# Opening of a fused pooling trunk: stores queued later, loads in another order, the second half's tiles one by one, small root steps on GpSimd

## The chip, the cores and the metric

The kernel runs on one core of a Trainium2 chip. TensorE (PE) multiplies, with its weight loads on a queue of their own (PEld); VectorE (DVE) and ScalarE (ACT) work on tiles in SBUF and PSUM; GpSimd (POOL) issues some DMAs and can do small arithmetic; SyncE (SP) issues the other DMAs. Each engine takes its own instructions in order, and waits are by semaphore. The metric is the device time of one execution in microseconds; lower is better. Three runs of the kernel before gave 965.98, 966.9 and 967.35 us, a median of 966.9.

## The reference

With DEPTH = 1 only the pooling mixer runs. Its input x is (1, 4096, 1024) in float32.

```
normed = x * rsqrt(mean(x*x, axis=-1) + 1e-6) * norm_w
u, gate = split(normed @ in_w, 2)                      # in_w 1024 x 2048
pooled  = trailing means of u, windows 2/4/8/16 for its four channel groups, minus u
mixed   = per group: pooled @ group_w + group_b        # four maps of 256 x 256
y       = mixed * scale * silu(gate)
h       = x + y @ out_w                                # out_w 1024 x 1024
out     = h * rsqrt(mean(h*h, axis=-1) + 1e-6) * final_norm_w
```

## The kernel before

**Weights.** The group map is linear and commutes with pooling, so the kernel folds it into the first matrix: `fold` (L329) multiplies the u columns of in_w by the group maps, 8 matmul chunks of 16 matmul records each, and writes the result out of PSUM scaled by norm_w (L346). Four chunks (group pair 0) stay in SBUF as `v0` and `v1`; the four chunks of group pair 1 go to DRAM (`wvd`, L955) and are read again much later.

**Products.** Each big product is one level of a seven-product scheme (P1 to P7): the 1024-wide contraction and the tokens are cut in halves, and combinations of the halves are multiplied. A block is 1024 tokens, in two halves of 512. `xs[b]` holds four pairs of input tiles: "11" and "12" are the first half (two contraction halves), "21" and "22" the second, each of two tiles of 128 x 1024. Float32 accuracy comes from two float32r parts: `split` (L153) writes the high part by ACT and the low part by DVE, and `mm3` (L509) makes three matmuls of each pair of parts. There are 48 matmuls in a product of the stages "a" and "b". The list of steps is a P1 P2 P6 P7 P5 P4 P3 for four blocks, then "b" likewise for the other half of the columns, then "o" with out_w.

**The opening** (L897 to L1023) is written out by hand and then ordered by a scheduler, so the lists of instructions on each engine are fixed in the built program. It holds 14 warming matmuls (L900), the 8 chunks of `fold`, P1 and P2 of block 0 on the raw input, and the row statistics of block 0. The statistics go as follows: x is read a second time by rows (`load_row` L354, four tiles for each half); ACT squares and sums them (`square_row` L361, L365); `stats` (L370) makes the mean square; `rsqrt` (L187) makes its inverse root, by an ACT square root, a DVE reciprocal and one Newton step of four small DVE instructions; `spread_rs` (L383) splits the result in two parts `hl`, multiplies an identity by them on DVE (L389) and lets PE spread them over all partitions by two matmuls with ones into bank 7 (L396); ACT copies that into `rstd` (L401). The scratch tile of L389 is w[P7][0], the place of one of P7's weights. The first half's spread stands inside P1 and the second half's inside P2 in PE's list. P1's and P2's results are multiplied by rstd when they leave PSUM (L623); P6 is the first product that needs normalized input, of both halves: `normalize_raw` (L497) for "11" and "12", L984 for "21" and "22", then `form_in` (L460) takes differences, `split_step` splits them, and P6 can run. Tiles of the first block that are needed again are saved to DRAM by POOL's queue (L429 and L501, eight stores, beside four of `wvd`).

**Buffers.** `st` and `vt` are rings of 128 x 1024 tiles. `early` and `early5` are views of the places of weights that come later (P4 and P3, and P5). SP's DMAs use eight semaphores in turn, so that a DMA waits at least for the one eight places ahead of it.

Lines that the change and the prediction touch: `rsqrt` L187, `fold` L329, `spread_rs` L383, `split_halves` L423, `normalize_raw` L497, `mm3` L509, `product_in` L518, the opening L917 to L989, and the first turn of the main loop, L1074.

Of the kernel before, what the change touches and what calls it, by code (L numbers as in the profile page):

```python
# [10 lines left out]
F32 = mybir.dt.float32  # L11
# [49 lines left out]
def kernel(  # L61
# [125 lines left out]
    def rsqrt(dst, tmp, ms):  # L187

        nc.scalar.activation(tmp, ms, AF.Sqrt)
        nc.vector.reciprocal(out=dst, in_=tmp)  # L190
# [137 lines left out]

    def fold(q, k, g, r, ps2, o, on_vector=False):  # L329

        for kk in range(2):
            for j in range(2):
                for t in range(2):
                    nc.tensor.matmul(  # L334
                        ps2[kk][:, j * 256 : (j + 1) * 256],
                        r[:, kk, 2 * j + t, :],
                        g[:, 2 * j + t, :],
                        start=(t == 0),
                        stop=(t == 1),
                    )  # L340
            if on_vector:
                last = nc.vector.tensor_scalar(
                    out=o[:, kk], in0=ps2[kk], scalar1=norm_c[k + kk], scalar2=None, op0=ALU.mult
                )
            else:
                last = nc.scalar.activation(o[:, kk], ps2[kk], AF.Copy, scale=norm_c[k + kk])  # L346
        give(r)
        return last

# [30 lines left out]
    def store_rs(b, half, rs):  # L380
        nc.sync.dma_start(out=rd[b][half][0].rearrange("(p j) -> p j", j=4), in_=rs)

    def spread_rs(half, rs):  # L383

        hl = small.tile([P, 2, 4], F32R, tag="hl", name=f"hl{half}")
        split(hl, rs)
        r = w[P7][0]
        for s in range(2):
            nc.vector.tensor_tensor(  # L389
                out=r[:, s, 0].rearrange("p (a j) -> p a j", j=4),  # L390
                in0=ident.rearrange("p a b -> p (a b)")[:, 0:P].unsqueeze(2).to_broadcast([P, P, 4]),
                in1=hl[:, s].bitcast(F32).unsqueeze(1).to_broadcast([P, P, 4]),
                op=ALU.mult,
            )
        for s in range(2):
            nc.tensor.matmul(  # L396
                banks[7], ones, r[:, s, 0], start=s == 0, stop=s == 1, skip_group_check=True
            )
        if half == 0:
            rstd[0] = take()  # L400
        copy(rstd[0][:, half], banks[7])  # L401
# [16 lines left out]
    def next_op(pattern, **sizes):  # L418
        t = ops[turn[0] % 4]
        turn[0] += 1  # L420
        return t.rearrange(pattern, **sizes)

    def split_halves(us, saved=None, by_pool=False):  # L423
        ts = []
        for h, u in enumerate(us):
            t = next_op("p (s a b) -> p s a b", s=2, a=2)
            split(t, u)
            if saved is not None:
                (nc.gpsimd if by_pool else nc.scalar).dma_start(out=saved[h], in_=u)  # L429
            ts.append(t)  # L430
        return ts
# [28 lines left out]
    def form_in(q, b, i):  # L460
# [6 lines left out]
        elif i == P6:  # L467
            s["2"] = [take(pool=early if q == 0 and b == 0 else None) for _ in range(2)]
            for h in range(2):
# [15 lines left out]
    def split_in(q, b, i):  # L485
# [9 lines left out]
        return t  # L495

    def normalize_raw(i):  # L497
# [9 lines left out]


    def mm3(ps, lt, r, start, stop):  # L509

        for n, (a, b) in enumerate(((lt[0], r[0]), (lt[0], r[1]), (lt[1], r[0]))):
            nc.tensor.matmul(  # L512
                ps, a, b, start=start and n == 0, stop=stop and n == 2, skip_group_check=True
            )

    bank_of = {P1: "x", P2: "x", P6: "y", P5: "y", P3: "y", P7: "v", P4: "v"}

    def product_in(i, t, sets, by_bank, between=None):  # L518
        ps = sets[bank_of[i]]
# [3 lines left out]
        for n, (h, ct) in enumerate(halves):  # L523
            if between and n in between:
                between[n]()
            c = slice(ct * P, (ct + 1) * P)
            for kk in range(2):
                mm3(
                    ps[ct],
                    (w[i][h][:, 0, kk, c], w[i][h][:, 1, kk, c]),  # L530
                    (t[h][:, 0, kk], t[h][:, 1, kk]),
                    i in (P1, P7) and h == 0 and kk == 0,
                    h == 1 and kk == 1,
                )

# [331 lines left out]

    def run(n, between=None):
        kind, b, i = steps[n]
# [4 lines left out]
        else:  # L874
            product_in(i, split_up.pop(n), sets, i == P1, between)
            evict_in(b, 0 if kind == "a" else 1, i, sets)
# [40 lines left out]
    for n, (h, k) in enumerate(chunks):  # L917
        if k < 4:
            o = v0[h] = take(pool=early)
        else:  # L920
            o = v1[h] = take()
        fold(0, k, gw[0], ru[0, k], banks[2 * (n % 2) : 2 * (n % 2) + 2], o)
        ru[1, k] = load_wut(1, k)
        if n == 0:
            load(0)
            g0.append(load_rows(in_w, 2, D))
            split_scaled(w[P1][0], g0[0], pair(norm_c, 0, 0))
        elif n == 1:
            split_step(0)
        elif n == 2:  # L930
            split_scaled(w[P1][1], g0[1], pair(norm_c, 1, 0))
# [20 lines left out]
    for n, (h, k) in enumerate(chunks):  # L952
        o = take(pool=early if n < 2 else early5)
        fold(1, k, gw[1], ru[1, k], banks[2 * (n % 2) : 2 * (n % 2) + 2], o)
        nc.gpsimd.dma_start(out=wvd[k // 2], in_=o)  # L955
        give(o)
        if n < 2:
            second_side(n)
            for j in range(2 * n, 2 * n + 2):
                square_row(0, 0, j)  # L960
            if n == 1:
                with tc.high_priority():
                    rs[0] = stats(0, 0)
        else:
            for j in range(2 * n - 4, 2 * n - 2):
                square_row(0, 1, j)
    give(gw[1])
    load(2)
    with tc.high_priority():
# [17 lines left out]
    run(1)  # L987
    normalize_raw(P2)
# [62 lines left out]
    for n in range(2, len(steps)):  # L1051
# [101 lines left out]
```

## Time and profile before

| what | value |
|---|---|
| median of three runs | 966.9 us |
| the profiled execution, its own time | 964.39 us |
| its span (first to last instruction) | 962.6 us |
| PE busy in the span | 949.7 us (99%), 4190 matmul records |
| DVE busy | 748.4 us (78%) |
| ACT busy | 453.0 us (47%) |
| POOL busy | 6.7 us, 16 instructions |
| granted TensorE clock, mean | 0.997 |
| one 128x512 matmul, L512, mean record | 389 ns |
| share of the busy 16 DMA engines, 10 to 60 us | 1.01 to 1.03 in each 10 us |
| the same, 70 to 80 us | 0.10 |

PE's records overlap, so the mean record is longer than the distance from one matmul to the next. PE is busy 844.55 of the 850 us from 110 to 960 us; most of what it stands idle lies in the first 62 us and after the last matmul. The trace shows 1.5 us of idle PE before its first matmul, and then waits of 1.2 us and 2.1 us in the opening. In the span's first 60 us the DMA engines have no pause, and from 40 to 80 us DVE has none either (9.92 of 10, then 10.00 of each 10 us).

### The profile page before, as it was taken

The page shows a single profiled execution, that of the slowest core. Times are in us where ns is not written, and L with a number is a line of the kernel's source. Part 1 is how long each engine was busy: PE and PEld are TensorE (multiplying, and loading weights), DVE is VectorE, ACT ScalarE, POOL GpSimd, SP SyncE. Part 2 cuts the span into 40 slices and gives each one's busy share as a digit, 9 for nine tenths or more (in the row PEclk, how much of TensorE's full clock was granted, in tenths as well). Part 3 has the DMA queues.
Part 4 walks back from the last instruction along what each step waited for, and adds up shares of the span by engine and source line. Part 5 has one row for each costly group of instructions (what it writes and reads, how often), then busy time and mean ns, then how long its engine had stood idle before and what let it go on. Part 6 is the DMA issues. An engine that isn't in the chain of part 4 may idle for free.

```text
span 962.6 us, 11058 instructions
## 1 busy us (share of the span) xinstructions
PE 949.7 (99%) x4190; PEld 785.5 (82%) x4190; DVE 748.4 (78%) x919; ACT 453.0 (47%) x677; POOL 6.7 (1%) x16
## 2 busy tenths in 40 slices
PE   9999999999999999999999999999999999999996
PEld 8778888888888888888888888888888888888885
DVE  4699994893895997696697599499978667677675
ACT  5849447347445555345345445553423424324233
POOL 0110000000000000000000000000000000000000
PEclk9999999999999999999999999999999999999998
DMA  9965864564656646016614733645746436356022
GB/s 337 408 264 157 305 237 163 210 240 137 213 219 226 233 156 237 1 45 218 240 44 165 263 119 131 219 151 178 259 141 212 162 123 230 108 187 218 22 88 88
DMA packets 67685, 177.01 MB, mean 184 GB/s; under 512 B 6704, under 2 KB 24240, under 8 KB 67632
## 3 DMA queue, kind: packets, MB, share of 16 engines
q1 hardware_dynamic: 61728, 156.37, 46.8%
q10 hardware_dynamic: 4176, 13.65, 3.5%
q0 software_dynamic: 1728, 6.29, 1.6%
q8 instruction: 33, 0.54, 0.2%
q14 instruction: 20, 0.16, 0.1%
HBM read 116.50 MB, written 59.78 MB: 183 GB/s over the span
## 4 chain that ended last, share of the span: by engine, by line
PE 78%; DVE 13%; DMA 5%; ACT 3%; issue 1%; DVEq 0%; SPq 0%; ACTq 0%
PE bank L512 75%; PE bank L334 2%; DVE op L145 2%; DVE vt L142 2%; DMA st<-wvd 2%; DVE st L148 1%; DVE st L145 1%; DMA rd<-rs 1%; DVE st L598 1%; DVE w L145 1%; DMA st<-rd 1%; DVE st L261 1%; DVE vt L145 1%; DVE w L209 1%; DVE st L142 1%
## 5 line engine op out<-in xcount | busy, mean ns | idle before, releaser
L512 PE MATMUL bank<-op,w 128*128 128x512 f32 x2688 | 611.7, 389 | 2.5 <-ACT op L151 2.1
L512 PEld LDWEIGHTS bank<-op,w 128*128 128x128 f32 x2688 | 504.0, 188 | 109.1 <-ACT op L151 2.6
L512 PE MATMUL bank<-w,op 128*128 128x512 f32 (+1 forms) x1356 | 305.0, 387 | 0.0
L512 PEld LDWEIGHTS bank<-w,op 128*128 128x128 f32 x1356 | 253.0, 188 | 52.0
L151 ACT ACTIVATE op<-st 128x1024 fp32r<-128x1024 f32 x117 | 123.2, 1056 | 142.0 <-PE bank L512 112.2
L145 DVE TENSOR_TENSOR op<-st,op 128x1024 fp32r<-128x1024 f32 x117 | 141.5, 1217 | 38.7 <-ACT op L151 38.3
L151 ACT ACTIVATE op<-vt 128x1024 fp32r<-128x1024 f32 x49 | 51.8, 1059 | 92.2 <-PE bank L512 72.9
L142 DVE TENSOR_TENSOR vt<-vt 128x1024 f32<-128x1024 f32 (+6 forms) x72 | 87.7, 1227 | 0.1
L142 DVE TENSOR_TENSOR st<-bank,st 128x512 f32<-128x512 f32 x78 | 53.1, 686 | 36.9 <-PE bank L512 36.6
L145 DVE TENSOR_TENSOR op<-vt,op 128x1024 fp32r<-128x1024 f32 x49 | 59.8, 1220 | 21.7 <-ACT op L151 21.7
L151 ACT ACTIVATE vt<-bank 128x512 f32<-128x512 f32 x90 | 52.6, 595 | 46.1 <-PE bank L512 42.5
L142 DVE TENSOR_TENSOR vt<-bank,vt 128x512 f32<-128x512 f32 (+1 forms) x83 | 55.1, 677 | 15.0 <-PE bank L512 10.8
L145 DVE TENSOR_TENSOR st<-st,st 128x1024 f32<-128x1024 f32 x35 | 42.3, 1217 | 13.0 <-DMA st<-wvd 11.2
L151 ACT ACTIVATE bank<-bank 128x512 f32<-128x512 f32 x44 | 25.5, 582 | 33.9 <-PE bank L512 30.1
L145 DVE TENSOR_TENSOR w<-st,w 128x1024 fp32r<-128x1024 f32 x22 | 26.5, 1220 | 16.4 <-ACT w L151 16.2
L148 DVE TENSOR_TENSOR st<-st,st 128x1024 f32<-128x1024 f32 (+1 forms) x18 | 20.4, 1160 | 19.6 <-DMA st<-rd 18.3
L151 ACT ACTIVATE w<-st 128x1024 fp32r<-128x1024 f32 x22 | 23.1, 1059 | 22.9 <-PE bank L512 15.4
L151 ACT ACTIVATE st<-bank 128x512 f32<-128x512 f32 x36 | 21.2, 596 | 21.1 <-PE bank L512 19.1
L593 DVE SCALAR_TENSOR_TENSOR vt<-vt,vt 128x1024 f32<-128x1024 f32 x24 | 29.2, 1217 | 0.1
L334 PE MATMUL bank<-early,early 128*128 128x256 f32 x128 | 27.8, 379 | 0.0
L334 PEld LDWEIGHTS bank<-early,early 128*128 128x128 f32 x128 | 24.3, 190 | 3.3
L598 DVE SCALAR_TENSOR_TENSOR st<-vt,colt,st 128x512 f32<-128x512 f32 x36 | 25.6, 742 | 0.0
(116 smaller groups left out, 449.7 us busy)
## 6 DMA issues: line engine op xcount, KB each, us to landing
st<-in_x SPq DMA_DIRECT2D x34, 512.0 KB, 4.5
vt<-in_x SPq DMA_DIRECT2D x25, 512.0 KB, 4.5
st<-sd SPq DMA_DIRECT2D x25, 512.0 KB, 5.4
st<-in_xt SPq DMA_DIRECT2D x24, 512.0 KB, 6.1
sd<-st ACTq DMA_DIRECT2D x19, 512.0 KB, 6.4
st<-yd SPq DMA_DIRECT2D x19, 512.0 KB, 3.7
yd<-st SPq DMA_DIRECT2D x18, 512.0 KB, 2.9
out<-st SPq DMA_DIRECT2D x17, 512.0 KB, 4.8
```

What stands on the lines that cost most here:

```text
L142: nc.vector.tensor_tensor(out=dst, in0=a, in1=b, op=ALU.add)
L145: nc.vector.tensor_tensor(out=dst, in0=a, in1=b, op=ALU.subtract)
L148: nc.vector.tensor_tensor(out=dst, in0=a, in1=b, op=ALU.mult)
L151: return nc.scalar.activation(dst, src, func)
L209: nc.vector.scalar_tensor_tensor(out=dst[:, 1], in0=u, scalar=c, in1=dst[:, 0].bitcast(F32), op0=ALU.mult, op1=ALU.subtract,)
L261: nc.vector.scalar_tensor_tensor(out=u[:, j], in0=u[:, j], scalar=cs[j], in1=other[:, j], op0=ALU.mult, op1=op)
L334: nc.tensor.matmul(ps2[kk][:, j * 256 : (j + 1) * 256], r[:, kk, 2 * j + t, :], g[:, 2 * j + t, :], start=(t == 0), stop=(t == 1),)
L512: nc.tensor.matmul(ps, a, b, start=start and n == 0, stop=stop and n == 2, skip_group_check=True)
L593: nc.vector.scalar_tensor_tensor(out=s[:, :, at : at + H], in0=s[:, :, at : at + H], scalar=1.0 / win, in1=v[:, :, HIST:], op0=ALU.mult, o ...
L598: nc.vector.scalar_tensor_tensor(out=sg[:, j], in0=s[:, j, at : at + H], scalar=bias_c[2 * grp + j], in1=sg[:, j], op0=ALU.add, op1=ALU.mult,)
```

## The change

It does five things, all of them in the opening, except that `rsqrt` is also used later.

1. The four small instructions of the Newton step in `rsqrt`, and the subtraction that makes the low part of `hl`, go from DVE to GpSimd. `rsqrt` is also used for blocks 1 to 3 and for the outputs (`finish`).
2. Stores: the four of `wvd` and the four of `normalize_raw` are no longer issued where the tiles are made but in step 2 of the main loop, behind the first of the four saves that P6 makes. The tiles of `wvd` stay held in P5's place until then.
3. Loads: the four rows of the first half are asked for before the last two chunks' weights, the inputs of P2 and its weights before the rows of the second half, and the inputs "21" and "22" right behind these.
4. In the second fold, one of the two evictions of each chunk goes from ACT to DVE; all four chunks use P5's place.
5. The spread of the second half goes to the end of P1 and is tied there (behind the latest matmul of P1), P2's second group of six matmuls is tied behind it, and P2 goes bank by bank. "21" and "22" are normalized, combined and split for the first contraction half before the second.

```diff
@@ rsqrt
-        mul(tmp, dst, ms)
-        mul(tmp, tmp, dst)
-        nc.vector.tensor_scalar(
+        nc.gpsimd.tensor_tensor(out=tmp, in0=dst, in1=ms, op=ALU.mult)
+        nc.gpsimd.tensor_tensor(out=tmp, in0=tmp, in1=dst, op=ALU.mult)
+        nc.gpsimd.tensor_scalar(
             out=tmp, in0=tmp, scalar1=-0.5, scalar2=1.5, op0=ALU.mult, op1=ALU.add
         )
-        mul(dst, dst, tmp)
+        nc.gpsimd.tensor_tensor(out=dst, in0=dst, in1=tmp, op=ALU.mult)
@@ fold: takes its own output tile
-            if on_vector:
-                last = nc.vector.tensor_scalar(
+        give(r)
+        o = take(pool=pool)
+        for kk in range(2):
+            if kk in on_vector:
+                nc.vector.tensor_scalar(
                     out=o[:, kk], in0=ps2[kk], scalar1=norm_c[k + kk], scalar2=None, op0=ALU.mult
                 )
@@ spread_rs
-        split(hl, rs)
+        copy(hl[:, 0], rs)
+        nc.gpsimd.tensor_tensor(
+            out=hl[:, 1], in0=rs, in1=hl[:, 0].bitcast(F32), op=ALU.subtract
+        )
...
-        for s in range(2):
-            nc.tensor.matmul(
-                banks[7], ones, r[:, s, 0], start=s == 0, stop=s == 1, skip_group_check=True
-            )
+        with tc.issue_after(latest[0]):
+            for s in range(2):
+                spread_done[0] = nc.tensor.matmul(
+                    banks[7], ones, r[:, s, 0], start=s == 0, stop=s == 1, skip_group_check=True
+                ).ins
@@ normalize_raw
-            nc.gpsimd.dma_start(out=sd[0][i][h], in_=u)
+            stores.append((sd[0][i][h], u))
@@ product_in
+            with tc.issue_after(behind) if behind and n == 1 else nullcontext():
+                for kk in range(2):
+                    mm3(
...
+        if between and 8 in between:
+            between[8]()
@@ first fold
-        if n > 1:
-            for j in range(2 * n - 4, 2 * n - 2):
-                load_row(0, 0, j)
+            ru[1, 4] = load_wut(1, 4)
+            for j in range(4):
+                load_row(0, 0, j)
...
-    for j in range(4):
-        load_row(0, 1, j, early if j < 1 else None)
     load(1)
     g1 = [load_rows(in_w, 4 + 2 * h, D) for h in range(2)]
+    for j in range(4):
+        load_row(0, 1, j, early if j < 3 else None)
+    load(2)
@@ second fold
-        o = take(pool=early if n < 2 else early5)
-        fold(1, k, gw[1], ru[1, k], banks[2 * (n % 2) : 2 * (n % 2) + 2], o)
-        nc.gpsimd.dma_start(out=wvd[k // 2], in_=o)
-        give(o)
+        o = fold(1, k, gw[1], ru[1, k], banks[2 * (n % 2) : 2 * (n % 2) + 2], early5, (0,))
+        stores.append((wvd[k // 2], o))
@@ block 0
-    run(0, {1: lambda: spread(0), 5: lambda: spread(1)})
+    run(0, {1: lambda: spread(0), 8: lambda: spread(1)})
...
+    s = xs[0]
+    s["2"] = [take(pool=early) for _ in range(2)]
+    split_up[2] = []
     for h in range(2):
         for key in ("21", "22"):
-            normalize(0, 1, xs[0][key][h])
-    form(2)
-    split_step(2)
-    run(1)
+            normalize(0, 1, s[key][h])
+        sub(s["21"][h], s["11"][h], s["21"][h])
+        sub(s["2"][h], s["22"][h], s["21"][h])
+        split_up[2] += split_halves([s["2"][h]])
+    run(1, behind=spread_done[0])
@@ main loop
         if n == 2:
+            with tc.issue_after(first_saves[0]):
+                for place, u in stores:
+                    nc.gpsimd.dma_start(out=place, in_=u)
+            for place, u in stores:
+                if id(u) in early5.used:
+                    give(u)
```

More of the change, by code (lines that the diff above doesn't have):

```diff
@@ L1 @@
 from collections import deque
-from contextlib import ExitStack
+from contextlib import ExitStack, nullcontext
 import numpy as np
@@ L428, in split_halves @@
             if saved is not None:
-                (nc.gpsimd if by_pool else nc.scalar).dma_start(out=saved[h], in_=u)
+                queue = nc.gpsimd if by_pool else nc.scalar
+                first_saves.append(queue.dma_start(out=saved[h], in_=u).ins)
             ts.append(t)
@@ L467, in form_in @@
         elif i == P6:
-            s["2"] = [take(pool=early if q == 0 and b == 0 else None) for _ in range(2)]
+            s["2"] = [take() for _ in range(2)]
             for h in range(2):
@@ L495, in split_in @@
         return t
+    stores = []
     def normalize_raw(i):
@@ L505, in form_s4, with product_in @@
             sub(u, u, s2)
+    latest = [None]
     def mm3(ps, lt, r, start, stop):
         for n, (a, b) in enumerate(((lt[0], r[0]), (lt[0], r[1]), (lt[1], r[0]))):
-            nc.tensor.matmul(
+            latest[0] = nc.tensor.matmul(
                 ps, a, b, start=start and n == 0, stop=stop and n == 2, skip_group_check=True
-            )
+            ).ins
     bank_of = {P1: "x", P2: "x", P6: "y", P5: "y", P3: "y", P7: "v", P4: "v"}
-    def product_in(i, t, sets, by_bank, between=None):
+    def product_in(i, t, sets, by_bank, between=None, behind=None):
         ps = sets[bank_of[i]]
@@ L866, in sets_of, with run @@
         return {"x": banks[0:4], "v": banks[0:4], "y": banks[4:8]}
-    def run(n, between=None):
+    def run(n, between=None, behind=None):
         kind, b, i = steps[n]
@@ L874, in run @@
         else:
-            product_in(i, split_up.pop(n), sets, i == P1, between)
+            product_in(i, split_up.pop(n), sets, i == P1 or behind, between, behind)
             evict_in(b, 0 if kind == "a" else 1, i, sets)
@@ L917 @@
     for n, (h, k) in enumerate(chunks):
[L918 to L923, printed above, removed]
+        v = v0 if k < 4 else v1
+        v[h] = fold(
+            0, k, gw[0], ru[0, k], banks[2 * (n % 2) : 2 * (n % 2) + 2], early if k < 4 else None
+        )
         if n == 0:
+            ru[1, 0] = load_wut(1, 0)
             load(0)
@@ L952 @@
     for n, (h, k) in enumerate(chunks):
-        o = take(pool=early if n < 2 else early5)
-        fold(1, k, gw[1], ru[1, k], banks[2 * (n % 2) : 2 * (n % 2) + 2], o)
-        nc.gpsimd.dma_start(out=wvd[k // 2], in_=o)
-        give(o)
+        o = fold(1, k, gw[1], ru[1, k], banks[2 * (n % 2) : 2 * (n % 2) + 2], early5, (0,))
+        stores.append((wvd[k // 2], o))
         if n < 2:
-            second_side(n)
             for j in range(2 * n, 2 * n + 2):
                 square_row(0, 0, j)
[L961 to L966, printed above, removed]
+            second_side(n)
+        if n == 1:
+            with tc.high_priority():
+                rs[0] = stats(0, 0)
     give(gw[1])
-    load(2)
+    for j in range(4):
+        square_row(0, 1, j)
     with tc.high_priority():
```

29 lines of the change are left out of this document (15 added, 14 removed).

## The prediction

> **What bounds the kernel now.** I read the table of stretches first, then PE's timeline, then the timelines of DVE, ACT and POOL from 20 to 63 us, and the lists of DMA issues. The columns of the first are stretch and length, then busy us of PE, PEld, DVE, ACT and POOL, granted clock, DMA share, GB/s.
> ```profile
> 6.40:34.20 27.80, 27.80 (x130) 24.48 (x129) 12.72 (x15) 21.22 (x32) 1.73 (x3) 1.00 1.02 384
> 34.20:48.40 14.20, 12.96 (x56) 10.02 (x56) 11.88 (x28) 10.90 (x21) 2.13 (x4) 1.00 1.03 417
> 48.40:58.75 10.35, 10.34 (x45) 7.99 (x44) 10.35 (x12) 3.55 (x4) 1.69 (x4) 1.00 1.03 412
> 58.75:62.32 3.57, 1.42 (x6) 0.86 (x6) 3.57 (x5) 3.48 (x4) 0.45 (x1) 1.00 0.95 388
> 62.32:115.25 52.93, 52.93 (x233) 43.75 (x234) 50.05 (x65) 37.48 (x57) 0.53 (x1) 1.00 0.59 194
> ```
> PE is full in the fold (6.4 to 34.2) and from 62.32 on; it stands idle in the second and fourth stretch. The granted clock is 1.00 in all of them, so it isn't a term. DVE is full from 48.4 to 62.32. PE's own lines name its waits:
> ```profile
> 36.80 0.50 PE L396 MATMUL bank<-w,w 128*128 128x512 f32 x1 [1.24 <-DVE w L389]
> 60.88 54.37 PE L512 MATMUL bank<-op,w 128*128 128x512 f32 x237 [2.14 <-ACT op L151]
> ```
> With 0.45 us more before the low part of P6's input (PEld at 62.32, behind DVE L145), that is 3.8 us. More can't be won in the opening, whatever the order. What sets the end is the DVE chain of the second half of x; its root steps:
> ```profile
> 42.43 0.17 DVE L190 RECIPROCAL rs<-tmp 128x4 f32<-128x4 f32 x1
> 46.77 0.16 DVE L148 TENSOR_TENSOR rs<-rs,tmp 128x4 f32<-128x4 f32 x1
> 47.57 1.29 DVE L389 TENSOR_TENSOR w<-early,hl 128x512 fp32r<-128x512 f32 x2
> 52.50 3.49 DVE L148 TENSOR_TENSOR st<-st,st 128x1024 f32<-128x1024 f32 x3
> 61.05 2.35 DVE L145 TENSOR_TENSOR op<-early,op 128x1024 fp32r<-128x1024 f32 x2
> ```
> Four steps need 4.3 us here, since each has a large operation behind it; DVE loses nothing by this, for it is never idle. After the spread come eight large operations, and at 62.27 the low part that P6 waits for.
>
> **The change, on DVE's chain.** I add up the changed kernel's DVE list with durations from before. 128x1024 counts 1.135 us from start to start (1.22 long), 128x512 from PSUM or for the spread 0.60 (0.69 long), scalar_tensor_tensor of 128x512 0.66 (0.75 long); ACT's 128x1024 1.05, its small copy 0.25 with the handover. Eight loads of 512 KB land between 15.86 and 26.34 in before, 1.31 us each, with the DMA engines full.
>
> Loads. The first half's rows move up one place and land at 22.5, 23.8, 25.1 and 26.3; ACT squares them one after another (1.05 and 0.19 each), the last at 27.9, so the mean square is there at 29.1 instead of 32.53. The price is the seventh chunk's weights, now behind the rows: 27.65 against 27.1, when PE gets there (6.41 + 6 x 3.45). PE then waits some 0.6 us; this costs nothing, as P2 waits later anyway. If that cover is gone it costs 0.6. The second half's rows land at 35.4 to 39.4 and the inputs "21" and "22" at 40.7 to 44.6, before their users (46.8 and later).
>
> First spread. On ACT a 128x1024 copy and the table load (1.28) stand before the square root; the reciprocal ends at 31.8. Now four steps on POOL. No arithmetic of POOL is in this trace, so a step is bounded by
> ```profile
> 0.24 0.10 POOL L1138 MEMSET const-float32-0.0<- 128x1 f32 x1 [0.24 <-issue]
> 54.13 0.54 POOL L429 DMA_DIRECT2D sd<-st  x1 [8.34 <-DVE st L148]
> 35.15 0.16 DVE L148 TENSOR_TENSOR tmp<-tmp,rs 128x4 f32<-128x4 f32 x1
> ```
> 0.10 from below and 0.54 from above; DVE's own chain of such steps goes by 0.20 each. I take 0.30 with the wait for the step before, near the middle and somewhat dearer than DVE. So 1.2 us to 33.1, ACT's high part 33.35, the two spread multiplications 33.4 to 34.6. PE reaches its spread after six matmuls of P1 at about 36, so the 1.24 us wait goes.
>
> Then DVE's list, without a wait: 6 x 1.135 (the low parts of P2's two inputs, four tiles normalized), 3 x 0.60 (one fold eviction, two banks), 5 x 0.66 (four weight parts, one combination): 11.9 us, to 46.5. Only now, by its place in the list, the mean square of the second half is made; its four squares on ACT (1.24 us each, with rows there by 39.4) are done before. A bank (0.60) covers the root on ACT; the reciprocal ends at 47.4. Of the four evictions moved to DVE (2.4 us) two fall in its idle time before 29 us, one under POOL's first steps, and one is in the 11.9.
>
> Second spread. The next on DVE are two scalar_tensor_tensor with both inputs in SBUF (L1029, 1.41 to the end of the second), which would cover POOL's steps. Whether POOL can work beside them no row shows. From the one side, the steps start at once: POOL 47.4 to 48.6, ACT 48.85, spread multiplications to 50.1. From the other, POOL and such a DVE operation exclude each other: POOL starts at 48.7 and ends at 49.9, ACT 50.15, the first multiplication to 50.9, the low part (POOL again, kept off by it) 51.2, the second to 51.9. I forecast the second. A row speaks for the later start too: beside a full DVE, POOL begins 0.40 us after the operation that releases it (the DVE operation of 55.91 ends at 57.13, the save starts at 57.53; again 58.26 and 58.67), where DVE follows itself at once. These are DMA issues, so I don't add it; where steps have it, the first time gets 0.4 at each reciprocal, and the second at the first reciprocal alone.
>
> [...]
>
> From the spread to P6's low part: spread matmul 0.50, ACT's high part of a weight 1.06 (it reuses the scratch tile), its low part on DVE 1.135, a bank 0.60, seven large ones 7.95, the split 1.22: 12.5 us. The one-by-one order saves less than it seems, because the weight's split went in front and three tiles of the second contraction half still stand before the low part. So it is done at 51.9 + 12.5 = 64.4, where before it was 62.27; four of P6's matmuls are done then instead of five, 0.23 us more. **Sum: +2.1 +0.23 = +2.4 us.**
>
> PE shows this as a wait of some 5 us inside P2 (four matmuls done at 47.1, the spread at about 52, everything else of P2 is tied behind it) and about 1 us in P6. All other PE waits behind it are the same as before: the next is 0.18 us at 127.3.
>
> Each 0.1 us of a POOL step is 0.8 to 0.9 us (eight steps on the chain, and the low part): with 0.10 the forecast is +0.6, with 0.54 +4.5.
>
> Stores. Twelve POOL issues at 0.53 leave between 57 and 67 us, among them eight that were spread over 24 to 67. DMA is at 1.02 until 60 and 0.10 from 70 to 80, so they have room. The first two saved tiles are overwritten by DVE at about 71; the first store would have landed at 70 by 5.9 us to landing and a queue of 1.3 us each: nothing, or 1 to 2 us if the queue is slower, half of which P5 and the following products can cover. Roots of blocks 1 to 3 and of the outputs become four POOL steps: 4 x (0.3 - 0.2) and two handovers, under 1 us each, with PE waiting for none of them. The last output rows use their own code, so the 7 us after the last matmul stay.
>
> **The rivals.** (a) POOL works beside DVE. Then the spread ends at 50.1, the low part at 62.6: +0.3 and +0.23, +0.6 us, 967.5; with 0.10 a step -1.0, 965.9; with 0.54 +2.4. This is the side of "not slower": the same chain, decided by whether the second half's steps start at 47.4 or 48.7. For it: POOL's DMA issues in before go on at 0.53 beside a full DVE. Against: those write no tile.
> (b) A step on POOL pays for its first use. The built list holds a library instruction ahead of the first step. The nearest row is ACT's load of a table at 33.21, 1.28 us; if it falls on the first spread, all behind it shifts: +2.4 + 1.28, 970.6. Against: the instruction waits for nothing and can be done long before 31.8.
> [...]
> (c) The stores are late: DVE's writes at 71 wait 1.5 us longer and PE is out of P5's input: +2.4 + 1.5, 970.8. For it: 6 MB in one queue. Against: the DMA share of 0.10 just behind.
> (d) Faster: under (a) all waits of DVE that I count go as well (0.9 before the first spread, 0.3 before the second, 0.9 behind it), which makes -1.5 us, and the 33 us of the chain go 2% quicker than by the rows of before, since eight stores no longer run beside it: -0.7 more, 964.7. Against: the large DVE operations take 1.22 us in before both at 57 us, with the stores, and at 69.65, without.
>
> **How the numbers follow.** The profiled execution took 964.39 us (span 962.6, 1.8 around it), 2.5 us under the median of 966.9; the sum is a difference on that execution, and I add it to the median: 966.9 + 2.4 = 969.3. 0.2%, what a measurement of this kernel can tell from no change, is 1.9 us. Forecast 0.47, (a) 0.33, (b) 0.05, (c) 0.05, (d) 0.10. The forecast lies from +0.6 to +4.5 by the step's price, about 0.30 of its 0.47 above 1.9; (a) is within 0.2% for 0.27, slower for 0.06. With (b) and (c): slower 0.46, within 0.44, faster 0.10, which I move to 0.48 and 0.42 for the late start. The range goes from (a) with the cheapest step and a little of (d), 965.5, to the forecast with a dear one and POOL's late start, 971.8; the forecast's own range is 967.5 to 971.4.
>
> **What would show it.** POOL's steps: their distance, and whether the first of the second half starts before or after L1029 ends on DVE. PE: no wait at the first spread, one of 3 to 5 us inside P2 and 1 us in P6 with the low part as its releaser; about 0.6 us in the fold's seventh chunk. DVE: the spread's second multiplication at 51 or at 49.5. I am wrong if P6's low part is done before 62 us, if POOL's steps are not on the chain, or if PE waits behind 65 us.

## The result, and the profile after

The changed kernel takes 971.07 us (median of six runs, 969.8 to 972.85); the kernel before took 966.44 us in six runs beside it. The ratio is 1.0048, with a 95% interval of 1.0033 to 1.0062: 4.6 us slower. The prediction said 969.3 us in a range of 965.5 to 971.8. So sign and range hold; but the sum was +2.4 us, all of it in the opening, and that is not where most of the 4.6 us lies.

PE's timeline of the changed kernel, as for the kernel before (start, length, engine, line, operation, tiles, count, then in brackets the idle time before it and what ended it):
```profile
7.50 28.11 PE L334 MATMUL bank<-early,early 128*128 128x256 f32 x128
36.84 0.62 PE L404 MATMUL bank<-w,w 128*128 128x512 f32 x2
51.35 0.50 PE L404 MATMUL bank<-w,w 128*128 128x512 f32 x1 [3.46 <-DVE w L396]
52.93 66.10 PE L527 MATMUL bank<-op,w 128*128 128x512 f32 x283
```
The first spread (36.84) has no wait any more, where it had 1.24 us. The second (51.35) has one of 3.46 us inside P2, where there was none. P6 has next to none: its low part is done at 64.55, and PE is there at 64.45. The waits of before, 1.24, 2.14 and 0.45, became one.

The same view from 110 us on, first of the changed kernel:
```profile
119.37 11.17 PE L527 MATMUL bank<-op,w 128*128 128x512 f32 x48 [0.34 <-DVE op L145]
130.72 66.98 PE L527 MATMUL bank<-op,w 128*128 128x512 f32 x294 [0.18 <-DVE op L145]
198.95 152.91 PE L527 MATMUL bank<-op,w 128*128 128x512 f32 x672 [1.25 <-DVE op L145]
352.64 20.72 PE L527 MATMUL bank<-op,w 128*128 128x512 f32 x90 [0.79 <-DVE op L145]
373.69 282.95 PE L527 MATMUL bank<-op,w 128*128 128x512 f32 x1247 [0.33 <-DVE op L145]
```
and of the kernel before:
```profile
127.32 239.66 PE L512 MATMUL bank<-op,w 128*128 128x512 f32 x1056 [0.18 <-DVE op L145]
367.17 282.96 PE L512 MATMUL bank<-op,w 128*128 128x512 f32 x1247 [0.19 <-DVE op L145]
```
Here are the new waits, 55 to 310 us behind the end of the opening: five in place of two, all for the low part of a split on DVE.

A table puts numbers to it. PE's matmuls come in a fixed number (14 to warm, 128 of the fold, 48 and 2, 48 and 2, then P6), so P6's tenth can be found in every profile. The first column is where the fold starts, the second from there to P6's tenth matmul, the third from there to the last matmul, and the fourth what the distances between matmuls in that stretch hold above 0.227 us. All are from one profile of each kernel, in us; the last column is the ratio to the kernel before in the timed runs.

| kernel | fold starts | to P6's tenth | P6's tenth to the last | waits in it | ratio [95%] |
|---|---|---|---|---|---|
| before | 6.41 | 56.95 | 891.29 | 0.99 | 1 |
| changed | 7.50 | 58.37 | 895.28 | 4.84 | 1.0048 [1.0033, 1.0062] |
| 1 later roots on DVE | 6.87 | 58.95 | 891.70 | 1.38 | 1.0005 [0.9992, 1.0018] |
| 2 all roots on DVE | 6.78 | 59.40 | 891.87 | 1.63 | 1.0009 [0.9998, 1.0019] |
| 3 stores as before | 6.37 | 64.47 | 899.63 | 9.18 | 1.0123 [1.0108, 1.0138] |
| 4 before, roots on GpSimd | 6.53 | 60.61 | 898.81 | 8.46 | 1.0115 [1.0083, 1.0147] |
| 5 changed, normalizations later | 6.07 | 57.88 | 891.17 | 0.95 | 1.0007 [0.9998, 1.0017] |
| 6 as 1, three things later | 6.17 | 54.95 | 891.58 | 1.38 | 0.9972 [0.9961, 0.9983] |
| 7 as 2, three things later | 7.01 | 53.72 | 892.48 | 2.25 | 0.9968 [0.9956, 0.9981] |
| 8 before, one thing later | 6.70 | 58.39 | 891.79 | 1.56 | 0.9996 [0.9986, 1.0005] |
| 9 as 7, rows as before | 7.33 | 55.24 | 894.51 | 4.31 | 1.0000 [0.9988, 1.0011] |
| 10 as 7, evictions as before | 6.66 | 54.49 | 893.56 | 3.29 | 0.9974 [0.9964, 0.9984] |
| 11 as 7, stores as before | 7.08 | 58.61 | 893.02 | 2.78 | 1.0023 [1.0013, 1.0032] |
| 12 as 7, combinations later | 6.52 | 53.70 | 891.17 | 0.97 | 0.9961 [0.9948, 0.9973] |

Between the two profiles, 4.0 us of the difference lie behind P6's tenth matmul, 1.4 in the opening, and 1.1 in the start of the fold, which changes from profile to profile (6.07 to 7.50, in no order) and isn't the change's. That is 6.5 us between the two profiled executions, where the medians differ by 4.6: the profile of the kernel before (964.39 us) is 2.0 us under its median, and that of the changed kernel (970.91) is at its own. So the parts from one profile each can be wrong by a microsecond or two, the opening's above all; the waits behind the opening are confirmed by the timed runs below.

### The profile page after: what moved, and what is told of

It reads as the page before. It is cut to its first block, busy times and chain, and to the rows that moved or that the text cites. A ratio compares the mean times of both kernels' runs of the same rounds, so it can differ in the third digit from the quotient of the medians.

```text
span 969.1 us, 11105 instructions
## 1 busy us (share of the span) xinstructions
PE 953.5 (98%) x4190; PEld 787.8 (81%) x4190; DVE 740.0 (76%) x833; ACT 448.1 (46%) x673; POOL 33.8 (3%) x106
## 4 chain that ended last, share of the span: by engine, by line
PE 70%; DVE 17%; DMA 6%; issue 2%; ACT 2%; POOL 1%; DVEq 0%; POOLq 0%; SPq 0%; ACTq 0%
PE bank L527 67%; DVE op L145 3%; DVE vt L142 2%; PE bank L334 2%; DMA rd<-rs 2%; DMA st<-wvd 2%; DVE st L148 2%; DMA st<-rd 1%; DVE st L145 1%; DVE vt L148 1%; DVE w L145 1%; DVE st L616 1%; DVE vt L145 1%; DMA sd<-vt 1%; DVE st L261 1%
## 5 line engine op out<-in xcount | busy, mean ns | idle before, releaser
L145 DVE TENSOR_TENSOR op<-st,op 128x1024 fp32r<-128x1024 f32 x117 | 142.4, 1223 | 50.9 <-ACT op L151 50.5
L142 DVE TENSOR_TENSOR vt<-vt 128x1024 f32<-128x1024 f32 (+6 forms) x72 | 88.2, 1235 | 0.2
L142 DVE TENSOR_TENSOR st<-bank,st 128x512 f32<-128x512 f32 x74 | 50.5, 689 | 34.7 <-PE bank L527 34.5
L151 ACT ACTIVATE vt<-bank 128x512 f32<-128x512 f32 x94 | 54.6, 595 | 43.7 <-PE bank L527 42.8
L142 DVE TENSOR_TENSOR vt<-bank,vt 128x512 f32<-128x512 f32 (+1 forms) x87 | 58.0, 680 | 14.8 <-PE bank L527 10.6
L145 DVE TENSOR_TENSOR op<-vt,op 128x1024 fp32r<-128x1024 f32 x49 | 59.8, 1224 | 9.7 <-ACT op L151 9.6
L145 DVE TENSOR_TENSOR st<-st,st 128x1024 f32<-128x1024 f32 x35 | 42.6, 1225 | 15.7 <-DMA st<-wvd 14.4
L148 DVE TENSOR_TENSOR st<-st,st 128x1024 f32<-128x1024 f32 (+1 forms) x17 | 19.2, 1156 | 22.9 <-DMA st<-rd 22.9
L145 DVE TENSOR_TENSOR w<-st,w 128x1024 fp32r<-128x1024 f32 x21 | 25.5, 1222 | 14.2 <-ACT w L151 14.0
L611 DVE SCALAR_TENSOR_TENSOR vt<-vt,vt 128x1024 f32<-128x1024 f32 x24 | 29.4, 1225 | 0.0
L191 POOL TENSOR_TENSOR otmp<-ors,oms 128x2 f32<-128x2 f32 x14 | 3.6, 259 | 661.7 <-DVE ors L190 661.7
L755 DVE SCALAR_TENSOR_TENSOR st<-st,ors,st 128x1024 f32<-128x1024 f32 x17 | 21.4, 1282 | 5.8 <-POOL ors L196 5.8
```

What stands on the lines that cost most here:

```text
L142: nc.vector.tensor_tensor(out=dst, in0=a, in1=b, op=ALU.add)
L145: nc.vector.tensor_tensor(out=dst, in0=a, in1=b, op=ALU.subtract)
L148: nc.vector.tensor_tensor(out=dst, in0=a, in1=b, op=ALU.mult)
L151: return nc.scalar.activation(dst, src, func)
L191: nc.gpsimd.tensor_tensor(out=tmp, in0=dst, in1=ms, op=ALU.mult)
L611: nc.vector.scalar_tensor_tensor(out=s[:, :, at : at + H], in0=s[:, :, at : at + H], scalar=1.0 / win, in1=v[:, :, HIST:], op0=ALU.mult, o ...
```

## The experiments

**1. Who makes the roots of the later blocks.** `rsqrt` gets its engine as an argument:
```diff
-        rsqrt(rs, tmp, ms)                       # stats
+        rsqrt(rs, tmp, ms, nc.gpsimd if b == 0 else nc.vector)
-        rsqrt(rs, tmp, ms)                       # outputs
+        rsqrt(rs, tmp, ms, nc.vector)
```


> The changed kernel, with the root steps of blocks 1 to 3 and of the outputs back on DVE; block 0 keeps them on GpSimd. In the changed kernel the profile has 4.6 us of PE waits behind 66 us (1.0 in the kernel before). Theory 1: they come from later root steps on GpSimd that DVE holds up (one took 3.36 us at 104 us). Then they fall to 1 to 1.5 us here and the time to about 967.5. Theory 2: they come from the order of DVE's list, which the scheduler made anew behind the changed opening. Then 4 to 5 us stay and the time is 970.5 to 971.5. Both: P6's first low part 57.1 us behind the fold's start, as in the changed kernel.

Measured: 967.51 us beside 967.16 for the kernel before, ratio 1.0005. The waits behind the opening fall to 1.38 us. So the later roots decide about 4 of the 4.6 us. (P6's low part, expected 57.1 us behind the fold's start, came at 57.6, after a wait of 2.40 us in the fold.) But theory 1 explains it by GpSimd's own time, and the trace speaks against that: the roots of block 2's second half leave for DRAM at 177.65 us in the changed kernel and at 182.60 here, so GpSimd is the earlier one, and yet PE waits at 198.95 only there. This is DVE in the changed kernel around the wait (timeline of DVE, lines between left out):
```profile
175.38 0.17 DVE L190 RECIPROCAL rs<-tmp 128x4 f32<-128x4 f32 x1
...
186.95 1.23 DVE L148 TENSOR_TENSOR st<-st,st 128x1024 f32<-128x1024 f32 x1 [5.49 <-DMA st<-rd]
188.09 1.22 DVE L611 SCALAR_TENSOR_TENSOR vt<-vt,vt 128x1024 f32<-128x1024 f32 x1
189.23 1.22 DVE L145 TENSOR_TENSOR op<-st,op 128x1024 fp32r<-128x1024 f32 x1
...
195.03 2.74 DVE L616 SCALAR_TENSOR_TENSOR vt<-vt,colt,vt 128x512 f32<-128x512 f32 x4
197.68 1.22 DVE L145 TENSOR_TENSOR op<-st,op 128x1024 fp32r<-128x1024 f32 x1
```
and the same stretch with later roots on DVE:
```profile
182.41 0.15 DVE L196 TENSOR_TENSOR rs<-rs,tmp 128x4 f32<-128x4 f32 x1
182.53 1.23 DVE L611 SCALAR_TENSOR_TENSOR vt<-vt,vt 128x1024 f32<-128x1024 f32 x1
183.67 1.22 DVE L145 TENSOR_TENSOR op<-st,op 128x1024 fp32r<-128x1024 f32 x1
184.81 1.88 DVE L142 TENSOR_TENSOR vt<-bank,vt 128x512 f32<-128x512 f32 x3
190.11 1.23 DVE L148 TENSOR_TENSOR st<-st,st 128x1024 f32<-128x1024 f32 x1 [3.42 <-DMA st<-rd]
```
The normalization (L148, `st<-st,st`) needs the root that comes back from DRAM. In the changed kernel the scheduler put it ahead of a pooling step (L611), a split (L145) and the bank additions (L142), which have all they need; they wait 5.49 us behind it, in order. With the root steps on DVE the list has it behind them, and they fill the time; the kernel before has the same order (its normalization at 186.04, behind a pooling step, a split and three bank additions). In the changed kernel the split at 197.68, PE's next input, then comes late. The wait near 200 us is in all three kernels that make the later roots on GpSimd and leave the order free (1.25 us here, 1.93 in experiment 3, 1.31 in experiment 4), and in none of the other profiles.

**5. Only that order.** Whether it is the order or GpSimd is told apart by moving the normalizations alone (four of 128x1024 in each of blocks 2 and 3), with GpSimd still making every root. `issue_after` queues what is made inside it behind the instruction that it names, here the last bank addition of the product before:
```diff
+                added[0] = nc.vector.tensor_tensor(out=u, in0=ps[c], in1=u, op=ALU.add).ins
...
-            normalize_a2(b)
+            with tc.issue_after(added[0]) if b > 1 else nullcontext():
+                normalize_a2(b)
```


> The changed kernel, GpSimd doing all root steps, with one thing: the normalization of the second half of blocks 2 and 3 is queued on DVE behind the last bank additions of the product before. In the changed kernel it stands ahead of the pooling step, a split and the bank additions, and DVE idles 5.5 us at 187 us for the roots to come back from DRAM; PE then waits 1.25 us at 199 us for a split. With the root steps of later blocks on DVE it stands behind them. If the order is the cause, the wait at 199 us goes and the PE waits behind the opening fall from 4.8 us to 3.5 or less, and the time by 1 to 3 us to about 969, though GpSimd still makes the roots. If GpSimd's own time is the cause, they stay at 4 to 5 and the time at 971.

Measured: 967.2 us beside 966.58, ratio 1.0007; the waits behind the opening are 0.95 us, and PE's view there has two small ones left (116.96 and 128.32, and none from there to the end of the stages "a" and "b"):
```profile
116.96 11.20 PE L527 MATMUL bank<-op,w 128*128 128x512 f32 x48 [0.26 <-DVE op L145]
128.32 522.30 PE L527 MATMUL bank<-op,w 128*128 128x512 f32 x2303 [0.16 <-DVE op L145]
```
On DVE the normalization now finds its root there (timeline, lines between left out):
```profile
181.05 2.48 DVE L667 TENSOR_TENSOR vt<-bank,vt 128x512 f32<-128x512 f32 x4
...
187.25 3.49 DVE L148 TENSOR_TENSOR st<-st,st 128x1024 f32<-128x1024 f32 x3
```
The gain was 4 us where 1 to 3 were expected: the waits at 350 and 370 us went as well. This settles it: of the 4.6 us about 4 are DVE's order in blocks 2 and 3. What is left, +0.6 us here and +0.35 in the first experiment, would be the opening's, but both intervals contain no change.

**2. The opening without GpSimd.** All steps of `rsqrt` and the low part of `hl` go back to `nc.vector`.

> The changed kernel with all root steps and the low part of hl on DVE; everything else as changed. DVE's list then has all four combinations of L1029 between the steps of the second half. If GpSimd's steps cost the opening what the profile shows (1.9 us from reciprocal to root, 0.4 of it by the exclusion, and 0.2 at each spread), DVE needs 0.8 for them but 2.65 for the combinations in between: P6's low part at 57.5 to 58.3 us behind the fold's start, against 57.1: moving the steps to GpSimd was not what cost the opening. If GpSimd is the main cost, it falls to 56 or less. The PE waits behind 66 us: 1 to 1.5 by theory 1 of the first experiment, 4 to 5 by theory 2.

Measured: 968.22 us, ratio 1.0009; P6's low part is ready 57.1 us behind the fold's start (63.83 less 6.78), as in the changed kernel (57.1), and the waits behind the opening are 1.63. So GpSimd neither costs nor brings anything in this opening that these runs can tell; the first of the two expectations has this side, though its 57.5 to 58.3 was somewhat late. GpSimd's steps are slower one by one (0.28 us from start to start in the first root of the changed kernel, 0.20 on DVE in that of the kernel before), but DVE puts the four combinations of L1029 between its own: from reciprocal to root it needs 2.9 us, GpSimd 1.9.

What GpSimd's steps cost is in its timeline of the changed kernel:
```profile
33.17 0.20 POOL L192 TENSOR_TENSOR tmp<-tmp,rs 128x4 f32<-128x4 f32 x1
33.46 0.19 POOL L193 TENSOR_SCALAR tmp<-tmp 128x4 f32<-128x4 f32 x1
...
48.50 0.62 POOL L191 TENSOR_TENSOR tmp<-rs,ms 128x4 f32<-128x4 f32 x1 [13.54 <-DVE rs L190]
49.19 0.58 POOL L192 TENSOR_TENSOR tmp<-tmp,rs 128x4 f32<-128x4 f32 x1
49.86 0.19 POOL L193 TENSOR_SCALAR tmp<-tmp 128x4 f32<-128x4 f32 x1
...
104.05 3.36 POOL L191 TENSOR_TENSOR tmp<-rs,ms 128x4 f32<-128x4 f32 x1 [17.61 <-DVE rs L190]
```
A step alone takes 0.20 us, 0.28 from start to start. The two at 48.50 and 49.19 stand beside the two scalar_tensor_tensor of L1029 on DVE (48.34, 1.38 us for both, where two of them take 1.41 in the kernel before) and end 0.06 us behind these, at 49.12 and 49.78. At 104.05 DVE has large operations with two inputs in SBUF without a gap (103.88 to 107.35), and one step took 3.36 us, to 107.41. DVE isn't held up in return: each multiplication of the spread takes 0.69 us here and in before. The two need 1.48 us instead of 1.29 because the second waits for its input, the low part of `hl`, which takes GpSimd 0.70 us beside the first.

**4. The kernel before, with only the roots on GpSimd.** The edit to `rsqrt` and `hl` of the change, nothing else.

> The kernel before, with only the root steps and the low part of hl on GpSimd, for all blocks. Theory 1 of the first experiment: PE waits behind 66 us grow from 1.0 to 3 or more, 969 or more. Theory 2: they stay within 1 us, and the opening changes by less than 1 us (the four steps, 4.3 us on DVE with large operations between, against four on GpSimd that each wait for one of these): 966 to 968.

Measured: 978.29 us, ratio 1.0115 [1.0083, 1.0147]. That is on the side of theory 1 (969 or more, waits of 3 or more; they are 8.46), but far more than either theory had a reason for. GpSimd's timeline there:
```profile
35.13 0.19 POOL L191 TENSOR_TENSOR tmp<-rs,ms 128x4 f32<-128x4 f32 x1 [2.71 <-DVE rs L190]
40.30 0.20 POOL L191 TENSOR_TENSOR tmp<-rs,ms 128x4 f32<-128x4 f32 x1 [4.97 <-DVE rs L190]
40.52 0.58 POOL L958 DMA_DIRECT2D wvd<-early  x1
41.12 2.28 POOL L192 TENSOR_TENSOR tmp<-tmp,rs 128x4 f32<-128x4 f32 x2
```
The first half's second step (41.12) stands behind the second half's first (40.30, which waits for DVE's reciprocal) and behind a store. The list is in order, so the first half's root, begun at 35.13, stands still for six microseconds. 3.7 us of the loss are in the opening and 7.5 behind it. Behind it DVE's list has the changed kernel's order: a normalization waits 6.47 us for its root at 189.52, and PE waits 1.31 us at 201.52. Two longer waits of PE, 2.01 us at 121.92 and 2.51 at 378.49, were not followed.

**3. The change with the stores where they were.**
```diff
-        stores.append((wvd[k // 2], o))
+        nc.gpsimd.dma_start(out=wvd[k // 2], in_=o)
+        give(o)
...
-            stores.append((sd[0][i][h], u))
+            nc.gpsimd.dma_start(out=sd[0][i][h], in_=u)
```


> The changed kernel with the stores of the folded weights and of P1's and P2's raw tiles issued where the tiles are made, as before. Theory A: the stores that stand together at 58 to 68 us delay what follows (a row's place, the second half of block 1), and cause the PE waits behind 66 us: these fall from 4.6 to 1 or 2 and the time to about 968. Theory B: they have room, the waits stay within 1 us of 4.6, and the time stays at 970 to 972.

Measured: 979.43 us, ratio 1.0123: neither theory; issuing the stores later doesn't cost, it saves some 7 us (1.0123 against 1.0048). Two stores of the folded weights, at 36.22 and 41.94, stand between the first half's steps on GpSimd's queue: the steps start at 34.70, 36.83, 42.54 and 43.33, and PE waits 5.39 us for the first spread, which had no wait in the changed kernel. Behind the opening there are 9.18 us of waits, 4.3 more than in the changed kernel; what makes these was not followed.

**11. The same without steps on GpSimd.** The same edit, on the version of experiment 7.

> The same version with the stores issued where the tiles are made. With the root steps on GpSimd this cost 12 us in the third experiment, where steps stood behind stores on GpSimd's queue. Here no step is on GpSimd. Theory 1: it was the queue; then the stores cost nothing here, within 1 us of 963. Theory 2: it was the place of the folded weights, which is taken anew when its store has landed (each some 6 us), so that the fold waits: still 3 us or more, 966 or more, with PE waits in the fold.

Measured: 968.52 us, ratio 1.0023 against 0.9968: 5.3 us, and the profiles have 4.9 more in the opening (58.61 against 53.72). So the queue is not the only reason; theory 2 has its line in DVE's timeline:
```profile
32.88 0.75 DVE L349 TENSOR_SCALAR early<-bank,colt 128x512 f32<-128x512 f32 x1 [3.17 <-DMA wvd<-early]
```
When a folded chunk's place is given back at its store, the next chunk takes the same place and its eviction waits for the store to land; PE then waits 1.38 us in the fold, 1.05 behind it and 1.96 at the second spread, none of which version 7 has. In the kernel before, two of the four chunks had another place. Whether both reasons add up in experiment 3 wasn't tried.

**6 and 7. A shorter chain to P6.** If DVE's chain sets the opening's end, what P6 doesn't need should leave it. Experiment 6 does this with later roots on DVE, 7 with all of them there:
```diff
+    p6_low = low[0]          # last low part that split has written: P6's
...
-    normalize_raw(P2)
+    with tc.issue_after(p6_low):
+        normalize_raw(P2)
...
+    with tc.issue_after(p6_low):
         for h in range(2):
             split(w[P7][h], v0[h])
...
+                    with tc.issue_after(p6_low):
                         nc.vector.scalar_tensor_tensor(out=g1[h][:, j], ...)
```


> The changed kernel with the root steps of later blocks on DVE (first experiment), and three things of DVE that P6 doesn't need queued behind P6's low parts: the normalization of P2's two raw tiles (2.3 us), the combinations of L1029 (2.65), the split of P7's weight (1.1, and 1.1 on ACT). Theory: the opening is DVE's chain to P6's low part, so it gets shorter by 3 to 4 us, the wait in P2 falls under 1 us and the one in P6 goes; PE is then full from P1 on, and the time is 964 to 965.5, faster than both. If the opening is bound elsewhere (by loads or PE's own work), 966 to 968.

> As the run before it, with all root steps on DVE, block 0's too. With the combinations out of the way nothing stands between the steps of the second half: 0.8 us on DVE against 1.2 on GpSimd, and the low part of hl 0.2 against 0.7. Theory: the same time within 0.5 us, or up to 1 us faster if the spread still sets the end; GpSimd brings nothing to the opening. If freeing DVE of ten small instructions matters, it is 0.5 to 1 us slower.

Measured: 963.69 us (ratio 0.9972) and 962.95 us (0.9968), both faster than the kernel before, the first a little more than expected. P6's tenth matmul comes 54.95 and 53.72 us behind the fold's start, 3.4 and 4.7 earlier than in the changed kernel. In experiment 6, where none of L1029's combinations stands beside the eight steps, each takes 0.19 to 0.20 us: the 0.62 and 0.58 above were DVE's company.

**8. One thing later in the kernel before.** `normalize_raw(P2)` behind P6's low parts.

> The kernel before, with only the normalization of P2's raw tiles queued behind P6's low parts: one of them (1.135 us) stands in the second half's root chain there. Theory of the DVE chain: P6's low part 0 to 1.1 us earlier (two things move into the place: a weight's split of P7 in front), 966 to 967. A gain of more than 1.5 us would mean that the chain is bound otherwise.

Measured: 966.22 us beside 966.58, ratio 0.9996: no change. A weight's split (50.72 in its profile) moved into the free place, so DVE's chain is no shorter: P6's low part is 56.7 us behind the fold's start, 55.9 in before.

**9 and 10. Two parts undone in version 7.** The first half's rows again two behind each of the last chunks' weights, and the eviction of the second fold by ACT alone (`early5, ()`).

> The version with all root steps on DVE and three things queued behind P6's low parts (963.0), with the first half's rows asked for behind the last chunks' weights again. In that version PE waits 0.8 us at 27.5 us for the seventh chunk's weights. Theory 1: the earlier rows are needed: they bring the mean square at 30 us instead of 33, and DVE's chain is bound from there on; without them the chain is 2 to 3 us later, 965 to 966. Theory 2: the chain is bound by DVE's other work and the fold's wait costs more than the rows bring: 962 to 963.

> The same version with the eviction of the second fold back on ACT alone. Theory 1: two of the four evictions moved stand on DVE's chain (1.2 us) and ACT has room: 0.5 to 1.2 us faster, about 962. Theory 2: ACT is full there (evictions, squares, high parts), so its high parts come later and DVE waits for them: 0.5 to 1.5 us slower, about 964.

Measured: 966.0 us without the early rows, 3 us behind version 7 (ratio 1.0000 against 0.9968), which is theory 1's time; but only half of it is in the opening (55.24 against 53.72), where theory 1 has all of it, and half is behind it (waits of 4.31 against 2.25, one of 2.73 us at 86 us for a high part on ACT). And 963.31 us with the evictions on ACT, ratio 0.9974: no difference that these runs can tell, so neither theory is shown.

**12. The combinations still later.** Made in `rest_of_first(P7)`, behind P5's low parts.

> The same version with the combinations of L1029 made one product later, behind P5's low parts. In that version PE waits 0.7 us at 83 us for P5's low part, with the combinations ahead of it. Theory: that wait goes, 962 to 962.5, if nothing behind it comes late; the same time within 0.3 us if P4's weights take its place.

Measured: 962.33 us, ratio 0.9961 [0.9948, 0.9973]; the lowest median, 4.2 us under the kernel before (966.5), though the interval doesn't part it from version 7's 0.9968. Its PE timeline, from the second spread to the end of the stages "a" and "b" (two lines between left out):
```profile
46.59 0.47 PE L408 MATMUL bank<-w,w 128*128 128x512 f32 x1
...
47.59 315.65 PE L531 MATMUL bank<-op,w 128*128 128x512 f32 x1391
363.94 282.95 PE L531 MATMUL bank<-op,w 128*128 128x512 f32 x1247 [0.70 <-DVE op L158]
```
All waits of the opening from P1 on are gone, as is the one at 83 us. What is left is 0.57 us in the fold and 0.70 at 364.

## Why the prediction was right, and where not

**The loads and the first spread: right.** The rows were forecast to land at 22.5 to 26.3 and land at 22.96 to 26.82; the mean square was forecast at 29.1, and is at 30.17 with a fold that starts 1.1 us later; the first spread's wait went. That the early rows matter at all is experiment 9. The seventh chunk's weights were to be 0.6 us late: PE's wait for them is nearly nothing in this profile, 0.57 to 0.71 us in experiments 2, 7, 11 and 12, 1.27 to 1.64 in 3, 5, 6 and 10, and PE waits 2.40 at this place in the first. Where PE waits in P2 later, it stays hidden, as forecast; in experiments 6, 7, 10 and 12 that cover is nearly gone.

**A POOL step at 0.30 us: right** (0.28 from start to start), except for the two steps beside L1029.

**POOL and L1029 exclude each other: half right.** The forecast let POOL start when both were done, root at 49.9, 2.5 us behind the reciprocal; rival (a) had 1.2. No row of before showed which of the two holds, so the 1.3 us between them were the author's estimate. It was 1.92 (48.42 to 50.34), 0.8 more than the first root with a fold eviction beside it (1.12, 32.82 to 33.94). In this trace POOL starts at once (48.50), and each of its two longer steps ends 0.06 us behind one of DVE's two: 0.62 and 0.58 us against 0.20 alone, while DVE loses nothing that shows (1.38 us for the two, 1.41 in the kernel before).

**DVE's chain: right.** 11.9 us were counted between the first spread and the second half's mean square, and it is 12.0 (35.60 to 47.58); 12.5 us from the spread to P6's low part, and it is 12.5 (52.1 to 64.55). The low part was forecast at 64.4 and is at 64.55, though the fold began 1.1 us late, so 0.9 us less than forecast when counted from there (57.1 against 58.0). Most of these 0.9 us lies in the two terms between reciprocal and spread: the root took 1.92 us for 2.5, and the spread behind it 1.75 for 2.0. The opening's +2.4 us is then mis-sized: +1.2 by P6's low part (57.1 against 55.9 behind the fold's start), +1.4 by P6's tenth matmul, and +0.35 and +0.6, not clear of nothing, in the timed runs of experiments 1 and 5.

**PE's waits in P2 and P6: too long.** Some 5 and 1 us were forecast, 3.46 and 0.16 came. By the prediction's own sum the first multiplication ends at 50.9, and PE's spread can start then, 3.8 us behind 47.1; the 5 us were counted to the end of the second. Some 1.4 us more (six matmuls of 0.227) went into slower matmuls, which the prediction didn't have: see the last section. It cost nothing, since P6's low part was the end.

**"All other PE waits behind it are the same as before": the step that failed.** They were 4.84 us instead of 0.99. And with it the sentence that roots of later blocks cost under 1 us each "with PE waiting for none of them": one step alone took 3.36 us. GpSimd's time was still harmless there, as experiment 5 shows. The working followed DVE's list up to P6 and the stores and took the rest for unchanged but for the steps themselves; yet with the steps off DVE's list the scheduler put other DVE operations in another order too, the normalization ahead of the pooling step.

**The rivals.** (a), POOL unhindered beside DVE, is ruled out by the 0.62 us, though its start at once is what came; of POOL's late start of 0.4 us nothing is seen (its first steps begin 0.08 us behind the reciprocal). (b), a dear first step, is ruled out by the first step's 0.20 us (32.90); whether anything was paid earlier, at the library instruction, no row shows. Of (c), late stores, nothing is seen: DVE's writes from 72.56 on don't wait; the stores' new place is what keeps GpSimd's queue free and the fold's places from being waited for. (d) didn't happen. So it was luck that the time came so near the range's upper end and stayed inside it: the opening was forecast some 1 to 2 us too dear and the 4 us behind it were missing, and the two errors went against each other. With the forecast's +2.4 us in the opening, the 4 us would have made about 973, outside the range.

## What to carry to other kernels

When small operations leave an engine, compare the whole list of that engine, not the place of the edit: a scheduler that no longer sees them may put a waiting operation ahead of ready ones, hundreds of microseconds on (here as far as 310 us behind the opening). An engine with a queue in order is only free for a short dependent chain if nothing that waits stands in between, other chains' steps and stores included (in experiment 4 a root begun at 35.13 stood still until 41.12). And where one engine's chain sets the end, taking out of it what the next product doesn't need (here 6 us of work) was worth more than moving its small steps elsewhere.

## What the runs showed of the hardware

**A wait of PE can slow what follows.** Windows of the changed kernel around its wait, then of experiment 5 (columns as in the prediction's table of stretches):
```profile
47.90:51.35 3.45, 0.00 (x0) 0.00 (x0) 2.51 (x5) 0.29 (x2) 2.29 (x5) 1.00 0.03 13
51.35:55.35 4.00, 4.00 (x11) 3.10 (x12) 3.10 (x5) 2.60 (x3) 0.01 (x1) 0.57 0.40 121
```
```profile
47.54:49.93 2.39, 0.39 (x3) 0.00 (x1) 1.44 (x3) 0.21 (x1) 1.82 (x5) 1.00 0.03 12
49.93:53.93 4.00, 4.00 (x17) 3.18 (x18) 3.60 (x6) 2.49 (x3) 0.00 (x0) 1.00 0.42 125
```
Behind 3.46 us of idle PE the granted clock was 0.57 over the next 4 us, with 11 matmuls instead of 17; behind about 2 us (here, and 2.14 in the kernel before) it stayed at 1.00. Behind 4.06 us (experiment 4) it was 0.59, behind 5.39 (experiment 3) 0.50. For a length between 2.14 and 3.46 us there are PE's rows of experiment 1: the fold's last 32 matmuls took 8.68 us behind a wait of 2.40, where they took 7.14 behind 0.71 in experiment 2.

**The fold's start moves by itself.** It lies between 6.07 and 7.50 us in the fourteen profiles, as the warming matmuls, 0.427 us apart at first, reach 0.23 apart earlier (from 5.0 us on in the kernel before) or later (only with the fold, from 7.2 us on, in the changed one); the last seven of them take 1.92 us in experiment 3, 1.96 in the kernel before and 3.05 in the changed one. One profile of each kernel can differ by 1.4 us for this alone; the runs of one kernel spread over 1.4 us (experiment 12, five runs) to 6.1 (experiment 4, four runs).
